# A mixer tile's gate products on VectorE: moved from ahead of the softmax maxima to behind them

## The chip, the cores and the metric

The kernel runs on one core of a Trainium2 chip. The metric is the device time of one execution in microseconds (us); it was measured in three runs, and one more execution was recorded by the hardware profiler. Engines are named as the profile names them: PE (TensorE's matmuls), PEld (its weight loads), DVE (VectorE), ACT (ScalarE), POOL (GpSimd), SP (SyncE, which issues most DMAs).

## What is computed

One decoder layer over 1024 tokens of width 1024, in f32. A first sub-layer mixes tokens: one input projection feeds (A) sliding-window attention of 8 query heads over 2 key heads (window 128, learned sinks) and (B) gated linear attention with 4 heads of 64 by 128. Their outputs are concatenated, projected and added to the input. A second sub-layer is a mixture of 32 experts, 4 for each token. Both are wrapped in norms and in shifts, scales and gates that come from a conditioning vector. The part that the change touches, cut from the reference:

```
s = jnp.where(valid, einsum(q, k) * scale, -inf)          # (A), a block of 128 tokens
m = jnp.maximum(jnp.max(s, -1), sink)
p = jnp.exp(s - m);  p = p / (sum(p) + jnp.exp(sink - m));  o = p @ v
...
b = jnp.cumsum(g, axis=2)                                  # (B), chunks of 64 tokens
A = einsum(q * jnp.exp(b - b_mid), k * jnp.exp(b_mid - b)) # masked to causal
o = A @ v + (q * jnp.exp(b)) @ states
kv = einsum(k * jnp.exp(b_last - b), v)                    # what a chunk adds to the state
```

## The kernel before

The program has three stretches: the projections of all tokens into the layouts that the mixer wants; a loop over eight tiles of 128 tokens that does both attentions (lines 682 to 719, about 164 to 392 us of the profiled span); and then the output projection, the router and the experts. Weights and activations of the big products are kept as a high and a low f16 half, so that one product is three matmuls (lines 149 to 151). Only the loop is touched.

A tile of the loop is written in this order. `gla_gates(t)` (line 534) makes the log gates (matmul L537, ACT L539 to L541, DVE L542), sums them within the chunks (matmul L546, ACT L552), takes differences on DVE (L553, L554) and exponentials on ACT (L555 to L558), and then, as its last part, multiplies the exponentials into the tile's queries and keys on DVE: ten instructions at L560 (a copy of the chunks' last decays), L563 (twice), L567 (four times), L570 (twice) and L573. They are called the products below. `project(t)` (line 509) makes the tile's linear-attention values and output gates: 96 matmuls into two PSUM buffers `pb`; the second goes through ACT L526, DVE L527, ACT L528 and L529, DVE L530. `ada_half(t)` (line 634) is POOL's work on the conditioning weights (L643 to L650), fed by DMAs that SP issues. `attention(t)` (line 456) has the scores in two rounds of four heads (matmuls L469 and L470), each round in two PSUM buffers `pss`; DVE adds the mask and takes the row maximum, head by head (L474); three short DVE instructions make the negative maximum and the sink's exponent (`nm` at L478 and L479, `es` at L481); ACT takes eight exponentials (L486). Then four rounds of transposes on PE (L495), copies out of PSUM by DVE (L501) or ACT (L499), products with the values (L504), and the division (L506). `gla(t)` (line 576) starts with the matmuls of the products with each other (L584, L585), masked copies on DVE (L588, L590), the matmuls L593 and L596, then the update of the state (L601 to L610) and the norm (L615 to L618).

Who sets the order: the source is traced, and the framework's scheduler then lays out one fixed queue for each engine, with the order of the source as priority and its own estimate of durations to decide what is ready. On the chip every queue runs in that order, and an instruction that has to wait holds up all behind it. The pool `psS` has two buffers `pss`, handed out in the order of the source: two for the gates of a tile, two and two for the rounds of scores, two for L584 and L585, one for the state's update. `tc.issue_after(ins)` adds to every instruction traced inside the block that is on the engine of `ins` an edge that puts it behind `ins` in that engine's queue.

Of the kernel before, what the change touches and what calls it, by code (L numbers as in the profile page):

```python
# [49 lines left out]
def layer_kernel(  # L50
# [4 lines left out]
    nc = tc.nc  # L55
# [118 lines left out]
    with tc.tile_pool(name="p1", bufs=1) as p1, tc.tile_pool(name="stage", bufs=4) as stage, \  # L174
# [211 lines left out]
        for t in range(NT):  # L386
            ps = psB.tile([128, 512], F32, name="pb")
            tk = slice(t * 128, (t + 1) * 128)
# [31 lines left out]
    with tc.tile_pool(name="p2", bufs=1) as p2, tc.tile_pool(name="wk", bufs=2) as wk, \  # L420
# [9 lines left out]
        sinkb = snk.rearrange("p i g -> p (i g)")  # L430
# [22 lines left out]
            for j in range(T, T + DUMP, 128):  # L453
                nc.sync.dma_start(yacc[j:j + 128, i * 512:(i + 1) * 512], am[0].rearrange("p a n -> p (a n)"))

        def attention(t, ao):
            w = 256 if t else 128
            k0 = (t - 1) * 128 if t else 0
            mx = wk.tile([128, 8], F32, name="mx")
            sms = []  # L460
            for i2 in range(2):
                sm = wk.tile([128, 4, 256], F32, name="sm")
                sms.append(sm)
                pss = [psS.tile([128, 2, 256], F32, name="pss") for _ in range(2)]
                for a in range(2):
                    for g in range(2):
                        i = 2 * i2 + a
                        tq, tk = slice(t * 128, (t + 1) * 128), slice(k0, k0 + w)
                        nc.tensor.matmul(pss[g][:, a, :w], qq[:, g, i, tq], kk[:, g, tk], start=True, stop=False)  # L469
                        nc.tensor.matmul(pss[g][:, a, :w], qq[:, g, i, tq], kl[:, g, tk], start=False, stop=True)  # L470
                for g in range(2):
                    for a in range(2):
                        h = 2 * (2 * i2 + a) + g
                        nc.vector.tensor_tensor_reduce(  # L474
                            sm[:, 2 * a + g, :w], pss[g][:, a, :w], amask[:, 256 - w:], op0=OP.add, op1=OP.max,
                            scale=1.0, scalar=-3e38, accum_out=mx[:, h:h + 1])
            nm = wk.tile([128, 8], F32, name="nm")
            nc.vector.scalar_tensor_tensor(nm, mx, SQK, sinkb, op0=OP.mult, op1=OP.max)  # L478
            nc.vector.tensor_scalar(nm, nm, -1.0, None, op0=OP.mult)  # L479
            es = wk.tile([128, 8], F32, name="es")  # L480
            nc.vector.tensor_add(es, sinkb, nm)  # L481
            nc.scalar.activation(es, es, AF.Exp)
            den = wk.tile([128, 8], F32, name="den")
            for h in range(8):
                sm = sms[h // 4][:, h % 4, :w]
                nc.scalar.activation(sm, sm, AF.Exp, scale=SQK, bias=nm[:, h:h + 1], accum_out=den[:, h:h + 1])  # L486
            nc.vector.tensor_add(den, den, es)
            rec = nc.vector.reciprocal(den, den)
            nk = w // 128
            po = psO.tile([128, 8, 64], F32, name="po")  # L490
            for i in range(4):
                pt = psT.tile([128, 4, 128], F32, name="pt")
                for g in range(2):
                    for b in range(nk):
                        nc.tensor.transpose(pt[:, g * nk + b, :],  # L495
                                            sms[i // 2][:, 2 * (i % 2) + g, b * 128:(b + 1) * 128], identf)
                pT = wk.tile([128, 4, 128], F32, name="pT")
                if i % 2:
                    nc.scalar.activation(pT[:, :2 * nk, :], pt[:, :2 * nk, :], AF.Copy)  # L499
                else:  # L500
                    nc.vector.tensor_copy(pT[:, :2 * nk, :], pt[:, :2 * nk, :])  # L501
                for g in range(2):
                    for b in range(nk):
                        nc.tensor.matmul(po[:, 2 * i + g, :], pT[:, g * nk + b, :],  # L504
                                         vv[:, t - nk + 1 + b, g * 64:(g + 1) * 64], start=b == 0, stop=b == nk - 1)
            nc.vector.tensor_tensor(ao, po, den[:, :, None].to_broadcast([128, 8, 64]), op=OP.mult)  # L506
            return rec

        def project(t, row):

# [23 lines left out]
        def gla_gates(t):  # L534
# [21 lines left out]
            nc.scalar.activation(ee[:, 0, :], ee[:, 0, :], AF.Exp)  # L556
            nc.scalar.activation(ee[:, 4, :], ee[:, 4, :], AF.Exp)
            nc.scalar.activation(bf, bf, AF.Exp)  # L558
            e3 = wk.tile([128, 2, 2], F32, name="e3")
            nc.vector.tensor_copy(e3.rearrange("p a c -> p (a c)"), ev[:, 2, :, 63])  # L560
            qk = ee.rearrange("p e (a n) -> p e a n", a=2)
# [9 lines left out]
                                        e3[:, :, 1 - c:2 - c].to_broadcast([128, 2, 64]), op=OP.mult)  # L571
            e4 = wk.tile([128, 2], F32, name="e4")
            nc.vector.tensor_tensor(e4, e3[:, :, 0], e3[:, :, 1], op=OP.mult)  # L573
            return ee, e4

        def gla(t, ee, e4, gv, sgg, go):
            A = am[t % 2]
# [104 lines left out]
        for t in range(NT):  # L682
            tk = slice(t * 128, (t + 1) * 128)
            row = ada_row(t // 2 - 1) if t and t % 2 == 0 else []

            wo = []
            for pc in range(t * 2, t * 2 + 2):
                cs = slice(pc % 8 * 128, (pc % 8 + 1) * 128)
                st = wos.tile([128, 4, 128], F32, name="wo", bufs=2)
                if pc >= 8:  # L690
                    wod = nc.sync.dma_start(st, w_out[512:1024, cs].rearrange("(i p) f -> p i f", p=128))
                else:
                    for g in range(2):
                        wod = nc.sync.dma_start(st[g * 64:(g + 1) * 64],
                                          w_out[g * 256:(g + 1) * 256, cs].rearrange("(i p) f -> p i f", p=64))
                ks = slice(pc // 8 * 4, pc // 8 * 4 + 4)
                wo.append((woh[:, ks, cs], wol[:, ks, cs], st))
            ao = wk.tile([128, 8, 64], F32, name="ao", bufs=1)
            gates = gla_gates(t)
            gv, sgg = project(t, row)  # L700
            with tc.issue_after(wod.ins):
                ada_half(t)
            rec = attention(t, ao)
            with tc.issue_after(rec.ins):
                for w in wo:
                    split(*w)
            aof = ao.rearrange("p h d -> p (h d)")
            pt = psT.tile([128, 4, 128], F32, name="pt")
            for i in range(4):
                nc.tensor.transpose(pt[:, i, :], aof[:, i * 128:(i + 1) * 128], identf)  # L710
            nc.scalar.activation(hTh[:, 0:4, tk], pt, AF.Copy, scale=SX)
            nc.vector.scalar_tensor_tensor(hTl[:, 0:4, tk], pt, SX, hTh[:, 0:4, tk], op0=OP.mult, op1=OP.subtract)
            go = wk.tile([128, 4, 128], F32, name="go", bufs=1)
            gla(t, *gates, gv, sgg, go)
            pt = psT.tile([128, 4, 128], F32, name="pt")
            for i in range(4):
                nc.tensor.transpose(pt[:, i, :], go[:, i, :], identf)
            nc.scalar.activation(hTh[:, 4:8, tk], pt, AF.Copy, scale=ggc)
            nc.vector.scalar_tensor_tensor(hTl[:, 4:8, tk], pt, ggc, hTh[:, 4:8, tk], op0=OP.mult, op1=OP.subtract)
# [764 lines left out]
```

## Time and profile before

| | us |
|---|---|
| three runs, median (lowest to highest) | 1987.58 (1984.33 to 1992.88) |
| the profiled execution, own time | 1980.73 |
| its span in the profile | 1978.6 |
| PE busy in the span | 1813.5 |
| DVE busy in the span | 1558.1 |

The span is the part that the profiler's records cover; 2.1 us of the profiled execution lie around it. All times inside the trace are from the span's start. A busy share says little of the whole here, since the stretches have different limits; what the change is worth has to be read from the loop.

### The profile page before, as it was taken

What the parts mean: (1) busy time and instruction counts of PE and PEld (TensorE: products, weight loads), DVE (VectorE), ACT (ScalarE), POOL (GpSimd) and SP (SyncE); (2) the same over time, 40 slices, a digit from 0 to 9 for tenths busy, and PEclk for the clock granted to TensorE, in tenths of its full rate; (3) what the DMA queues carried; (4) which work ended last, traced back from release to release, by engine and by line L of the source; (5) the groups of instructions that cost most, each with busy time, mean ns of one, the idle gap of its engine ahead of it and who ended that gap; (6) DMA issues with size and microseconds to landing.
All of it is one profiled execution on the core that took longest, in us unless ns stands there. A gap on an engine that the chain in (4) does not pass through costs nothing. (4 is left out here: it accounts for less than half of the span.)

```text
span 1978.6 us, 55425 instructions
## 1 busy us (share of the span) xinstructions
PE 1813.5 (92%) x22803; PEld 1587.7 (80%) x22803; DVE 1558.1 (79%) x2568; ACT 1305.4 (66%) x2247; POOL 1007.2 (51%) x989
## 2 busy tenths in 40 slices
PE   6999999989598999999999999999999999999980
PEld 3456887755398999999999997779889998999880
DVE  6824667666689989998998995779697978989873
ACT  5624555434376978878788785668577768868760
POOL 2204777646545656456565574436344535754441
PEclk9999999999699999999999999999999999999985
DMA  9412333333499999999999997689888989999983
GB/s 298 151 44 75 97 87 102 112 136 128 168 366 330 353 350 304 370 354 317 349 356 365 361 347 251 225 306 348 284 315 289 372 266 347 359 307 348 313 276 107
DMA packets 296630, 525.79 MB, mean 266 GB/s; under 512 B 19056, under 2 KB 79611, under 8 KB 296340
## 3 DMA queue, kind: packets, MB, share of 16 engines
q1 hardware_dynamic: 277682, 476.27, 69.1%
q0 software_dynamic: 17392, 41.72, 8.9%
q8 instruction: 180, 2.95, 0.6%
q10 hardware_dynamic: 1298, 4.21, 0.5%
q14 instruction: 78, 0.64, 0.1%
HBM read 482.37 MB, written 39.76 MB: 264 GB/s over the span
## 5 line engine op out<-in xcount | busy, mean ns | idle before, releaser
L171 DVE SCALAR_TENSOR_TENSOR el<-st,eh 128x1024 f16<-128x1024 f32 x768 | 934.7, 1240 | 91.2 <-ACT eh L170 89.2
L170 ACT ACTIVATE eh<-st 128x1024 f16<-128x1024 f32 x768 | 794.2, 1055 | 238.0 <-PE pu L150 133.6
L149 PE MATMUL pu<-xTh,eh 128*128 128x232 f16 (+31 forms) x4096 | 778.8, 231 | 7.6 <-DVE lin L1129 5.2
L150 PE MATMUL pu<-xTl,eh 128*128 128x232 f16 (+31 forms) x4096 | 777.8, 230 | 5.1 <-issue 4.9
L151 PE MATMUL pu<-xTh,el 128*128 128x232 f16 (+31 forms) x4096 | 777.9, 230 | 4.2 <-issue 4.2
L150 PEld LDWEIGHTS <-eh 128*128 128x128 f16 x6080 | 595.1, 99 | 42.0 <-issue 20.2
L149 PEld LDWEIGHTS <-eh 128*128 128x128 f16 x6080 | 592.8, 98 | 28.5 <-issue 6.6
L151 PEld LDWEIGHTS <-el 128*128 128x128 f16 x6080 | 592.5, 98 | 28.7 <-issue 6.8
L1132 POOL CAST aTh<-lin 128x232 f16<-128x232 f32 (+31 forms) x256 | 295.0, 1153 | 476.0 <-DVE lin L1131 411.0
L149 PE MATMUL pyv<-aTh,eh 128*128 128x232 f16 (+30 forms) x1984 | 375.4, 231 | 10.7 <-ACT yT L1159 6.7
L151 PE MATMUL pyv<-aTh,el 128*128 128x232 f16 (+30 forms) x1984 | 374.9, 231 | 1.5 <-issue 1.5
L150 PE MATMUL pyv<-aTl,eh 128*128 128x232 f16 (+30 forms) x1984 | 374.8, 230 | 0.8 <-issue 0.8
L1133 POOL TENSOR_TENSOR aTl<-lin,aTh 128x232 f16<-128x232 f32 (+31 forms) x256 | 271.2, 1060 | 20.6
L1129 DVE TENSOR_SCALAR lin<-pu,bt 128x232 f32<-128x232 f32 (+31 forms) x256 | 109.9, 429 | 71.8 <-PE pu L151 58.7
L1174 POOL DMA_INDIRECT yacc<-yo,tokI x52 | 94.4, 1815 | 114.7 <-ACT yo L1171 108.2
L1125 ACT ACTIVATE gl<-pu,bt 128x232 f32<-128x232 f32 (+31 forms) x256 | 98.1, 383 | 65.8 <-PE pu L151 35.1
L1130 DVE SCALAR_TENSOR_TENSOR lin<-lin,bt,sg 128x232 f32<-128x232 f32 (+31 forms) x256 | 105.2, 411 | 18.6 <-ACT sg L1127 4.6
L643 POOL TENSOR_TENSOR st<-st,sil 128x512 f32<-128x512 f32 x64 | 69.1, 1080 | 94.1 <-DMA st<-in_w_ada_dram 92.6
L1127 ACT ACTIVATE sg<-gl,c 128x232 f32<-128x232 f32 (+31 forms) x256 | 108.0, 422 | 1.0
L1087 POOL DMA_INDIRECT xg<-h2d,gatI x50 | 71.4, 1428 | 43.8 <-DVE gcol L1250 20.8
L1131 DVE SCALAR_TENSOR_TENSOR lin<-gl,lin 128x232 f32<-128x232 f32 (+31 forms) x256 | 83.6, 327 | 4.3
L1171 ACT ACTIVATE yo<-pxy,gcol 128x512 f32<-128x512 f32 (+26 forms) x104 | 70.3, 678 | 5.8 <-DMA yacc<-yo,tokI 5.8
(411 smaller groups left out, 2488.7 us busy)
## 6 DMA issues: line engine op xcount, KB each, us to landing
st<-in_w_mlp_dram SPq DMA_DIRECT2D x384, 1024.0 KB, 11.3
st<-in_w_ada_dram SPq DMA_DIRECT2D x64, 256.0 KB, 3.0
xt<-in_x_dram SPq DMA_DIRECT2D x16, 512.0 KB, 4.3
st<-in_w_ada_dram SPq DMA_DIRECT2D x16, 512.0 KB, 9.1
st<-in_w_in_dram SPq DMA_DIRECT2D x7, 1024.0 KB, 5.0
x1d<-xt SPq DMA_DIRECT2D x8, 512.0 KB, 2.6
h2d<-h2s SPq DMA_DIRECT2D x8, 512.0 KB
yacc<-yi ACTq DMA_DIRECT2D x8, 512.0 KB, 2.9
```

The source lines that it names most:

```text
L149: nc.tensor.matmul(ps, sh, mh, start=first, stop=False)
L150: nc.tensor.matmul(ps, sh, ml, start=False, stop=False)
L151: return nc.tensor.matmul(ps, sl, mh, start=False, stop=last)
L170: return (nc.scalar.activation(dh, src, AF.Copy, scale=SW), nc.vector.scalar_tensor_tensor(dl, src, SW, dh, op0=OP.mult, op1=OP.subtract))
L171: nc.vector.scalar_tensor_tensor(dl, src, SW, dh, op0=OP.mult, op1=OP.subtract))
L1125: nc.scalar.activation(gl, pu[0], AF.Relu, scale=-SG, bias=bc(0, j))
L1127: sgs.append(nc.scalar.activation(sg, gl, AF.Sigmoid, scale=-1.702 * INV / SG, bias=c7))
L1129: nc.vector.tensor_scalar(lin, pu[1], bc(1, j), bc(2, j), op0=OP.max, op1=OP.min)
L1130: nc.vector.scalar_tensor_tensor(lin, lin, bc(3, j), sg, op0=OP.add, op1=OP.mult)
L1132: nc.gpsimd.tensor_copy(aTh[:, j, :], lin)
L1133: lows.append(nc.gpsimd.tensor_tensor(aTl[:, j, :], lin, aTh[:, j, :], op=OP.subtract))
L1174: end["dma"] = nc.gpsimd.indirect_dma_start(out=yacc, out_offset=bass.IndirectOffsetOnAxis(ap=si(b)[:m, :], axis=0), in_=yo[:m, :], in_off ...
```

## The change

The ten products leave `gla_gates` and become a function of their own, `gla_products`, which `attention` calls behind `es`. They are thereby behind the tile's maxima in the source, so in priority, and `issue_after` puts them behind the `es` instruction of L481 in DVE's queue. No instruction is added or removed, no tile's size or number of buffers changes, no other engine's instruction is moved in the source.

```diff
-        def attention(t, ao):
+        def attention(t, ao, ee):
...
-            nc.vector.tensor_add(es, sinkb, nm)
+            top = nc.vector.tensor_add(es, sinkb, nm)
             nc.scalar.activation(es, es, AF.Exp)
+
+            with tc.issue_after(top.ins):
+                e4 = gla_products(t, ee)
             den = wk.tile([128, 8], F32, name="den")
...
-            return rec
+            return rec, e4
...
             nc.scalar.activation(bf, bf, AF.Exp)
+            return ee
+
+        def gla_products(t, ee):
+            tk = slice(t * 128, (t + 1) * 128)
+            ev = ee.rearrange("p e (a n) -> p e a n", a=4)
             e3 = wk.tile([128, 2, 2], F32, name="e3")
             nc.vector.tensor_copy(e3.rearrange("p a c -> p (a c)"), ev[:, 2, :, 63])
             qk = ee.rearrange("p e (a n) -> p e a n", a=2)
...
             nc.vector.tensor_tensor(e4, e3[:, :, 0], e3[:, :, 1], op=OP.mult)
-            return ee, e4
+            return e4
...
-            gates = gla_gates(t)
+            ee = gla_gates(t)
             gv, sgg = project(t, row)
             with tc.issue_after(wod.ins):
                 ada_half(t)
-            rec = attention(t, ao)
+            rec, e4 = attention(t, ao, ee)
...
-            gla(t, *gates, gv, sgg, go)
+            gla(t, ee, e4, gv, sgg, go)
```

## Rows read from the trace of the kernel before

**Rows 1.** The page's head: the span of the profiled execution.

```profile
span 1978.6 us, 55425 instructions
```

**Rows 2.** Windows: the eight tiles of the loop summed; the experts' stretch.

```profile
core 0: us, PE busy (x) PEld busy (x) DVE busy (x) ACT busy (x) POOL busy (x), PEclk, DMA share, GB/s
...
sum 227.60, PE 211.97 PEld 179.26 DVE 157.79 ACT 117.23 POOL 164.42; mean PE 26.50 PEld 22.41 DVE 19.72 ACT 14.65 POOL 20.55
...
545.00:1960.00 1415.00, 1337.40 (x19615) 1260.54 (x19613) 1213.44 (x1662) 1058.31 (x1604) 736.13 (x630) 0.98 0.95 322
```

**Rows 3.** Timeline of SP's queue: the first loads of expert weights.

```profile
527.50 3.54 SPq L1057 DMA_DIRECT2D st<-in_w_mlp_dram  x2
```

**Rows 4.** PE's waits in the loop, 164 to 392 us: total, times, longest.

```profile
PE pss L469 <- DVE mx L474: 8.4, 7, 2.5
PE pss L546 <- DVE az L542: 3.7, 3, 2.9
PE pt L495 <- ACT sm L486: 0.8, 3, 0.3
PE pt L677 <- DVE mx L675: 0.8, 1, 0.8
```

**Rows 5.** The first of these waits in tiles 3, 4, 5 and 7.

```profile
PE pss L469 <- DVE mx L474: 1.8, 1, 1.8
...
PE pss L469 <- DVE mx L474: 0.5, 1, 0.5
...
PE pss L469 <- DVE mx L474: 2.1, 1, 2.1
...
PE pss L469 <- DVE mx L474: 2.5, 1, 2.5
```

**Rows 6.** DVE timeline, tile 5: start, duration, line, operands, count, idle before.

```profile
309.61 0.67 DVE L563 TENSOR_TENSOR ee<-gkT,ee 128x256 f32<-128x256 f32 x1
...
311.22 1.12 DVE L570 TENSOR_TENSOR ee<-ee,e 128x128 f32<-128x128 f32 x1
...
314.16 0.41 DVE L527 TENSOR_SCALAR vg<-vg 128x512 f32<-128x512 f32 x1
```

**Rows 7.** PE timeline, tile 5: the second round of scores.

```profile
315.31 0.27 PE L469 MATMUL pss<-kk,qq 128*128 128x256 f16 x1 [2.09 <-DVE mx L474]
```

**Rows 8.** ACT timeline, tile 5: the activation ahead of L527.

```profile
311.51 0.60 ACT L526 ACTIVATE vg<-pb 128x512 f32<-128x512 f32 x1 [0.76 <-PE pb L151]
```

**Rows 9.** DVE timeline, tile 4, from the first product to the second copy.

```profile
281.78 0.60 DVE L563 TENSOR_TENSOR ee<-gkT,ee 128x256 f32<-128x256 f32 x1
...
284.06 0.28 DVE L570 TENSOR_TENSOR ee<-ee,e 128x128 f32<-128x128 f32 x1
284.26 0.15 DVE L573 TENSOR_TENSOR e<-e 128x2 f32<-128x2 f32 x1
...
285.84 0.80 DVE L527 TENSOR_SCALAR vg<-vg 128x512 f32<-128x512 f32 x1 [1.24 <-ACT vg L526]
...
290.68 0.44 DVE L588 COPY_PREDICATED am<-triu,pss 128x256 f32<-128x256 uint32 x1 [0.27 <-PE pss L585]
...
291.37 0.15 DVE L481 TENSOR_TENSOR es<-snk,nm 128x8 f32<-128x8 f32 x1
...
293.23 0.69 DVE L501 COPY pT<-pt 128x512 f32<-128x512 f32 x1 [0.55 <-PE pt L495]
295.68 0.69 DVE L501 COPY pT<-pt 128x512 f32<-128x512 f32 x1 [1.75 <-PE pt L495]
```

**Rows 10.** ACT timeline, tile 4: the first exponential.

```profile
291.22 0.51 ACT L486 ACTIVATE sm<-sm,nm 128x256 f32<-128x256 f32 x1 [3.25 <-DVE nm L479]
```

**Rows 11.** PE timeline, tile 4: the first reader of products, and a later one.

```profile
289.54 0.48 PE L584 MATMUL pss<-ee 64*128 64x128 f32 x2
...
295.91 0.61 PE L596 MATMUL po<-vg,am 128*128 128x128 f32 x4
```

**Rows 12.** POOL timeline, beside the slow L570 of tile 5.

```profile
311.11 1.08 POOL L643 TENSOR_TENSOR st<-st,sil 128x512 f32<-128x512 f32 x1 [1.11 <-DMA st<-in_w_ada_dram]
```

## The prediction

> **What bounds the kernel now.** I read the profile from the whole to the place. The span is 1978.6 us [rows 1], and the executed time of that execution 1980.73, so 2.1 us lie around it. The windows by stretch come next: in the eight tiles of the loop PE is busy 211.97 of 227.60 us, DVE only 157.79, ACT 117.23, POOL 164.42 [rows 2]. So the loop is bound by PE, which leaves 227.60 - 211.97 = 15.6 us idle, and nothing that is done to DVE can bring more than that there, unless PE's own work changed, which it does not. The experts' stretch is bound by PE too (1337.40 of 1415.00 us, [rows 2]); its first weights are issued at 527.50 [rows 3], 135 us behind the loop, behind routing that needs the loop's result. What the loop gains or loses therefore passes on to the end one for one.
>
> Then the view of PE's waits, cut to the loop, says what the idle time is [rows 4]: 8.4 us before L469, the second round of scores, which needs a `pss` buffer that the maxima of the first round still read; 3.7 us before L546, for the gates of the next tile; 0.8 and 0.8 us elsewhere. Together 13.7 us. The reader should see that the largest one is a wait for DVE, and that it is uneven: 1.8, 2.1 and 2.5 us in tiles 3, 5 and 7, but 0.5 us in tile 4 [rows 5].
>
> Why it is uneven stands in the timelines. In tile 5 DVE goes through the ten products from 309.61 to the start of L527 at 314.16, 4.55 us without a gap [rows 6]; the activation that L527 needs ended at 311.51 + 0.60 = 312.11 [rows 8], so L527 and the maxima behind it were 2.05 us late because of the products, and PE stood 2.09 us at L469 [rows 7]. In tile 4 the products took from 281.78 to 284.26 + 0.15 = 284.41, 2.63 us, and DVE then sat idle 1.24 us, waiting for ACT, ahead of L527 [rows 9]: there they were in nobody's way.
>
> **The change part by part.** *What is taken away from ahead of the maxima.* With the products gone, L527 of tile 5 starts at 312.11 and the maxima some 2.05 us earlier; L469, which started at 315.31 [rows 7], could start at 313.26, and PE had been idle since 315.31 - 2.09 = 313.22. The wait goes almost wholly. I take tiles 3 and 7 for the same pattern, since their waits are of the same size, and leave each tile the 0.5 us that tile 4 has with products that hindered nobody. Saved: 1.8 + 2.1 + 2.5 - 3 x 0.5 = 4.9 us. Bounds: nothing, if another thing is late next (it would be L526 itself, which waits for PE), and 8.4 us.
>
> *What is put behind `es`.* Ten DVE instructions in each of eight tiles, no DMA among them, and no other queue, SP's and POOL's included, has an instruction moved in the source. The cover is the time in which ACT takes eight exponentials: in tile 4 they begin at 291.22 [rows 10], `es` ends at 291.37 + 0.15 = 291.52, and DVE's copies for the transposes start at 293.23 and 295.68, with idle time before them [rows 9]. The masked copies L588 and L590, now partly between the maxima and `es`, must come behind the products, which brings `es` and the exponentials forward by about 0.6 us (0.44 us of L588 and 0.27 us of idle before it, [rows 9], less overlap). The ten then run from about 290.9 to 293.5 in tile 4's duration. The copy at 293.23 starts 0.3 us later; the products with the values behind it on PE wait as long, but PE has other work there. In tile 5's duration, 4.55 us, they end at 295.4, and the copy is 2.2 us late. DVE is not the bound, so its work as such costs nothing; if that cover is gone, it costs what PE waits.
>
> *The new wait.* L584 is the first reader of the products. It starts at 289.54 in tile 4 [rows 11], that is before `es`; now it can't start before about 293.5, 4 us later. Queued behind it on PE are the next tile's projection, the transposes and L596. The scheduler knows the dependency and fills PE with the 48 projection matmuls of the next tile that it now puts between, and L596 comes only at 295.91 [rows 11], so the 4 us are room that exists. What it does not know is how late DVE really is. Lower bound 0. Upper bound: the queue is laid out for durations like tile 4's, 2.63 us, and every tile takes tile 5's 4.55 us; then PE waits 4.55 - 2.63 = 1.9 us in each, 8 x 1.9 = 15.4 us. The nearest row is the wait for a result that comes out of the same place today, L495 for the exponentials: 0.8 us over the whole loop [rows 4]. I take 1 us.
>
> *What makes the products slow, and whether the new place cures it.* L570 of tile 5 started at 311.22, took 1.12 us [rows 6] and so ended at 312.34; POOL's L643 ran from 311.11 to 312.19 [rows 12]. The same line took 0.28 us in tile 4 [rows 9]: it was held until POOL was through, and then ran its usual length nearly. POOL is busy 164.42 of 227.60 us, 72% of the loop [rows 2], so a chain of ten meets it in the one place as in the other, and I count no change of its own from this. The Trainium skill, SBUF — State Buffer, section "SBUF: two separate sides", states the rule behind it: DVE with two inputs in SBUF and GpSimd share a pair of ports as an exclusive lock, and whoever comes second is blocked for the whole instruction. By that rule the ten are slow wherever POOL is at work, the late end of tile 5 would be the usual one, and the sum would be that of the second rival below; the rows show such holds in tile 5 and not in tile 4.
>
> *The sum.* -4.9 + 1.0 = -3.9 us. Against the profiled execution that is 1980.73 - 3.9 = 1976.8 us; this execution lies 6.9 us below the median of the runs shown, 1987.58, and the forecast is made against the median: 1987.58 - 3.9 = **1983.7 us**, 0.2% less.
>
> **The rivals.** A measurement of this kernel can tell about 0.5% from no change, 9.9 us.
>
> *All of PE's waits close.* With the maxima early, the whole tile moves forward, `az` (the 3.7 us) too, and PE runs without a named wait: -13.7 us, 1973.9. For it: DVE has 70 us free in the loop. Against it: the wait before L546 comes from work of the tile's end, which the change does not hurry, and tile 4 keeps 0.5 us with no product in the way.
>
> *The new wait takes the place of the old one, slower.* The place is L584 on PE, held by products that POOL holds up; PE's queue is in order, and tile 5 shows that it does not forgive 2 us of late DVE work [rows 6, 7]. The price is 15.4 us by the upper bound above, and the net -4.9 + 15.4 = +10.5: 1998.1 us. It turns from gain to loss where the wait is over 4.9 / 8 = 0.6 us in each tile, and it can be told from no change only where it is over (9.9 + 4.9) / 8 = 1.85 us. Against it: the scheduler may lay L584 out later than it must, and 4 us of projection stand ready.
>
> *The maxima do not come earlier.* The scheduler lays out PE's queue anew; it sees DVE free earlier, puts the second round of scores earlier too, and the wait stays as it is, for L527 and its ACT input: 0 us, 1987.6, or 1988.6 with the 1 us of the new wait. Tile 4 speaks for it, tiles 3, 5 and 7 against it.
>
> **How the numbers follow.** The forecast, a gain of some 1 to 8 us, gets 0.56; all waits closed 0.14; the slower one 0.15; no effect 0.15. Faster by over 0.5% is nearly all of the second case (0.13) and an upper end of the first (0.04): 0.17. Slower by over 0.5% is most of the slower case (0.12), and 0.02 for a layout that turns out worse in other ways: 0.14. The rest, 0.69, is within 0.5%. The range takes in the end of the closed waits (1973.9) and that of the slower rival (1998.1): 1973 to 1999; the likeliest case's own is 1979 to 1988.
>
> **What would show it.** In the profile of the changed kernel, PE's wait L469 <- L474 should fall from 8.4 to about 3.5 us, most in tiles 3, 5 and 7; the products should stand between L481 and the first L501 of each tile; the exponentials should start some 0.6 us sooner behind the maxima; a wait L584 <- product should be new and small, and L527 should follow L554 with only a wait for ACT between. I would be wrong if L584's wait were over 5 us in all, if PE's busy time in the loop changed, if the wait at L469 stayed, or if the time moved behind the loop, where I count nothing.

## The result, and the profile after

The median of the changed kernel is 2016.01 us (1994.87 to 2031.11, 13 runs), that of the kernel before, on the same chip, 1988.97 us (1977.60 to 1999.14, 13 runs): a ratio of 1.0113, interval 1.0089 to 1.0136. The ratio leaves out the three longest runs of the changed kernel (2025.13 to 2031.11 us), which lie over 1.5% above its fastest; the medians, with all runs, differ by 27.0 us. It is slower by more than the 0.5% that a measurement can tell, and outside the range given. The profiled execution took 2010.1 us, 29.4 more than that of before; the two lines of the page's head that matter are the span and the granted clock in 40 slices:

```profile
span 2008.3 us, 55412 instructions
...
PEclk9998888899869999999999999999999999999985
```

The loop has the whole of it. The timeline of SP's queue has the first load of expert weights at 559.25 instead of 527.50 us [rows 3], 31.8 later:

```profile
559.25 0.43 SPq L1065 DMA_DIRECT2D st<-in_w_mlp_dram  x1
```

Cut from the first difference of a tile's gates to the last writing of a mixer's result, the loop takes 258.9 us; cut in the same way it takes 227.4 us in the kernel before:

```profile
164.40:391.80 227.40, 211.76 (x1695) 179.18 (x1693) 157.59 (x459) 117.23 (x365) 164.42 (x261) 0.99 0.33 96
```

The windows of the kernel after, the loop first, then 14 us each from three of the falls described below, and 14 us of tile 3, where none came:

```profile
core 0: us, PE busy (x) PEld busy (x) DVE busy (x) ACT busy (x) POOL busy (x), PEclk, DMA share, GB/s
165.90:424.80 258.90, 241.76 (x1703) 203.32 (x1702) 156.71 (x459) 113.68 (x365) 163.54 (x261) 0.87 0.31 87
212.00:226.00 14.00, 13.48 (x60) 11.92 (x60) 5.61 (x14) 2.16 (x6) 6.61 (x10) 0.51 0.38 111
250.00:264.00 14.00, 13.84 (x62) 12.72 (x63) 5.12 (x11) 0.60 (x1) 8.47 (x11) 0.52 0.38 108
376.00:390.00 14.00, 14.00 (x63) 12.07 (x63) 5.77 (x17) 2.78 (x9) 6.27 (x11) 0.51 0.40 114
...
280.00:294.00 14.00, 12.37 (x97) 10.51 (x96) 8.72 (x21) 6.27 (x23) 5.66 (x8) 1.00 0.33 96
```

The reader should see two things. PE's busy time in the loop, 211.97 us in [rows 2], is now 241.76, with the same 22803 matmuls in the program: each takes longer. And the column PEclk says why. In the stretches from 212, 250 and 376 us it stands at 0.51 or 0.52, so nearly all of each ran at half clock (1.2 instead of 2.4 GHz), though PE is shown busy for 13.48 to 14.00 of 14 us; in the last row, of tile 3, PE is busy only 12.37 us and the clock is full. The clock record of the trace has five such stretches in the loop, called falls here: from 181.5 us for 10.2, and from 212.2, 249.8, 314.6 and 376.1 us for 13.7 each, 64.8 us in all. The kernel before had one of 3.4 us. If one half of the time at half clock is lost, that makes (64.8 - 3.4) / 2 = 30.7 us, against 258.9 - 227.4 = 31.5 measured. Reckoned at full clock, the two loops are about equally long: 258.9 - 32.4 = 226.5 and 227.4 - 1.7 = 225.7.

This holds beyond the one execution that was profiled, since every run has its span and its mean granted clock on record. Their product is the length that the span would have had at full clock throughout: its median is 1917.5 us in the 13 runs of the changed kernel (1909.4 to 1921.4) and 1914.6 to 1915.7 in the 74 runs of the kernel before that stood beside the experiments, on four chips. The spans themselves have medians of 2014.2 us against 1984.8 to 1988.8.

PE's waits in the loop, total, times and longest:

```profile
PE pss L593 <- DVE ee L575: 5.2, 5, 1.7
PE pt L498 <- ACT sm L489: 3.2, 6, 0.9
PE pss L469 <- DVE mx L474: 3.0, 5, 0.9
PE po L507 <- DVE pT L504: 2.3, 4, 1.1
PE pss L592 <- DVE ee L571: 1.9, 3, 1.3
PE pt L725 <- DVE go L626: 0.4, 1, 0.4
PE pss L549 <- DVE az L545: 0.2, 1, 0.2
```

The aimed-at wait went from 8.4 [rows 4] to 3.0 us, and that for `az` (now L549) from 3.7 to 0.2. But the first readers of the products (L592 and L593, before L584 and L585) wait 7.1 us, the products with the values 2.3, and the transposes (L498) 3.2 instead of 0.8. The sum is 16.2 against 13.7: even at full clock nothing was won.

Where a fall begins is seen in tile 2. DVE's timeline: start, duration, line, operands, count:

```profile
244.30 0.17 DVE L481 TENSOR_TENSOR es<-snk,nm 128x8 f32<-128x8 f32 x1
244.39 0.16 DVE L568 COPY e<-ee 128x4 f32<-128x4 f32 x1
...
245.13 1.33 DVE L575 TENSOR_TENSOR ee<-gkT,ee 128x128 f32<-128x128 f32 x2
246.38 0.81 DVE L578 TENSOR_TENSOR ee<-ee,e 128x128 f32<-128x128 f32 x1
247.11 1.59 DVE L575 TENSOR_TENSOR ee<-gqT,ee 128x128 f32<-128x128 f32 x2
...
249.43 0.68 DVE L504 COPY pT<-pt 128x512 f32<-128x512 f32 x1
```

POOL's timeline beside it:

```profile
244.94 1.17 POOL L651 TENSOR_TENSOR st<-st,sil 128x512 f32<-128x512 f32 x1 [1.43 <-DMA st<-in_w_ada_dram]
246.19 0.85 POOL L653 TENSOR_TENSOR st<-st 128x256 f32<-128x256 f32 x1
247.01 1.08 POOL L651 TENSOR_TENSOR st<-st,sil 128x512 f32<-128x512 f32 x1
```

PE's timeline, with the idle time before an instruction and its releaser in brackets:

```profile
246.25 0.38 PE L498 MATMUL pt<-identf,sm 128*128 128x128 f32 x2
248.29 0.44 PE L593 MATMUL pss<-ee 64*128 64x64 f32 x4 [1.67 <-DVE ee L575]
...
250.16 1.97 PE L507 MATMUL po<-vv,pT 128*128 128x64 f32 x8 [0.48 <-DVE pT L504]
...
255.40 3.52 PE L507 MATMUL po<-vv,pT 128*128 128x64 f32 x16
...
259.56 0.42 PE L151 MATMUL pb<-wvh,hTl 128*128 128x256 f16 x1
```

The two pairs of L575 took 1.33 and 1.59 us, where such a pair takes 0.48 to 0.53 with POOL cut (a_pool below). The first pair ended at 246.46, 0.35 us behind POOL's L651 (246.11), L578 at 247.19, 0.15 behind L653 (247.04), and the second pair at 248.70, 0.61 behind the next L651 (248.09): each got through only when POOL was done. So the products ran to 249.4 and longer; in the time that tile 4 had taken before, 2.63 us [rows 9], they would have ended at 247.0. PE stood 1.67 us before L593 and 0.48 before L507, and from 249.8 us the clock was at half: the eight L507 take 1.97 us and the f16 matmul 0.42, where the same took 1.10 and 0.27 at full clock. Six f16 matmuls came from 259.56, and at 263.4 the clock was back.

What PE did around these waits had changed as well. The scheduler's PE queue for one middle tile, one character for each matmul (`.` f16 projection, `s` attention scores, `G` L584 and L585 or their like, `t` transposes, `v` products with the values, `f` other f32 matmuls):

```
before: ssssssss........ssss...ssss........GGGG.GGGG....tt...tt..tt...tvvvvtttttffffvvvvvvvvttttff..vvvv........
after:  ssssssss........ssss...ssss......................tt.GGtt.ttGGttGGvvvvttttGGffvvvvvvvvtttt......vvvvfff
```

With the products late, the scheduler put 22 f16 matmuls in a row ahead of the transposes and had only two left for the passage behind them. From the first transposes to the next six f16 matmuls PE has, but for these two, only f32 matmuls in small tiles. This passage is called **the f32 run** below. A long row of them is not new: 32 stand there without any f16 matmul between them, and 28 did before. What is new is that the transposes and the products' readers ahead of that row have hardly any f16 matmul among them, where there had been a dozen, and that PE waits there.

### The profile page after: what moved, and what is told of

Its sections match the earlier page's. It is cut to its first block, busy times and chain, and to the rows that moved or that the text cites. A ratio compares the mean times of both kernels' runs of the same rounds, so it can differ in the third digit from the quotient of the medians.

```text
span 2008.3 us, 55412 instructions
## 1 busy us (share of the span) xinstructions
PE 1840.6 (92%) x22803; PEld 1608.8 (80%) x22803; DVE 1558.4 (78%) x2568; ACT 1301.9 (65%) x2247; POOL 996.0 (50%) x989
## 3 DMA queue, kind: packets, MB, share of 16 engines
q1 hardware_dynamic: 277682, 476.27, 68.3%
## 5 line engine op out<-in xcount | busy, mean ns | idle before, releaser
L1141 POOL TENSOR_TENSOR aTl<-lin,aTh 128x232 f16<-128x232 f32 (+31 forms) x256 | 257.8, 1007 | 20.6
L651 POOL TENSOR_TENSOR st<-st,sil 128x512 f32<-128x512 f32 x64 | 67.8, 1060 | 113.9 <-DMA st<-in_w_ada_dram 66.7
```

Source lines behind the costliest of these rows:

```text
L1141: lows.append(nc.gpsimd.tensor_tensor(aTl[:, j, :], lin, aTh[:, j, :], op=OP.subtract))
```

## The experiments

**Theory 1:** a fall needs both, the f32 run and a wait in it, and the waits come from products that POOL holds up. **The rivals:** the new order of PE's queue is enough by itself, or the waits are enough wherever they fall. The expectations have a third theory too, that the clock is a bystander and the chain of a tile has become longer. The loop is compared cut as above; *low* is its time at half clock by the clock record, and *at full* is its length less half of that.

| kernel | loop us | low us | at full | ratio to before (interval) |
|---|---|---|---|---|
| before | 227.4 | 3.4 | 225.7 | |
| after | 258.9 | 64.8 | 226.5 | 1.0113 (1.0089 to 1.0136) |
| a_pool | 214.7 | 0 | 214.7 | loop only |
| b_pool | 211.9 | 0 | 211.9 | loop only |
| b_late | 236.3 | 17.1 | 227.8 | 1.0014 (0.9985 to 1.0043) |
| a_split | 226.9 | 3.4 | 225.2 | 1.0007 (0.9983 to 1.0031) |
| a_dummy | 289.6 | 68.3 | 255.5 | 1.0161 (1.0111 to 1.0210) |
| a_reorder | 273.4 | 95.6 | 225.6 | 1.0108 (1.0054 to 1.0163) |
| a_weave | 236.8 | 23.9 | 224.9 | 1.0008 (0.9978 to 1.0039) |
| b_weave | 256.6 | 47.8 | 232.7 | 1.0142 (1.0088 to 1.0195) |
| b_half | 225.4 | 10.2 | 220.3 | 0.9979 (0.9949 to 1.0008) |
| b_dve | 232.7 | 17.1 | 224.2 | 1.0031 (1.0006 to 1.0056) |
| a_dve | 232.8 | 13.7 | 226.0 | 1.0069 (1.0038 to 1.0100) |
| a_weave_half | 230.0 | 13.7 | 223.2 | 1.0013 (0.9989 to 1.0037) |

The column *at full*, with the product of span and clock above, is the main evidence that the clock carries the difference, and it speaks against the third theory: where the conditioning is computed in full, it lies between 220.3 and 227.8 us in ten of twelve kernels, while the loop itself goes from 225.4 to 273.4. The two others (a_dummy, b_weave) have work or waits of their own. Each kernel was profiled once, so the loop of a single execution stands beside a ratio of several; where the two differ in size (a_reorder), the falls of other executions need not be those of the one profiled.

### a_pool: the changed kernel, POOL hardly there

POOL's conditioning products are cut to 8 of every 128 columns; the other columns are left out, so the router sends the tokens elsewhere and the stretches behind the loop are not compared.

```diff
+                    st = st[:, :, 0:8]
+                    acc = adac[:, pc * 128:pc * 128 + 8]
-                    nc.gpsimd.tensor_tensor(st, st, sil[...].to_broadcast([128, 4, 128]),
+                    nc.gpsimd.tensor_tensor(st, st, sil[...].to_broadcast([128, 4, 8]),
```

> The changed kernel with POOL's conditioning products cut to 8 of 128 columns (most of the conditioning is left out); the queues of PE and DVE keep the changed kernel's order. Theory 1 (waits): in the changed kernel PE waits 7 us in the loop for products that POOL holds up (L592, L593), inside a run of small f32 matmuls, and its clock falls to 1.2 GHz for some 13 us in five tiles; with POOL short the ten products take about 2.3 us, these waits fall under 2 us, the clock stays at 2.4 GHz in at least six of eight tiles, and the time is 1970 to 1988 us. Theory 2 (order): the clock falls because the f16 projection matmuls are used up ahead of a run of some 60 f32 matmuls, waits or not; it still falls in four or more tiles and the time stays 2003 to 2020 us. Theory 3 (chain): the clock is a bystander and the tile's chain is longer; the period of a tile stays above 30 us at full clock too.

The loop's window, with the columns of the windows above:

```profile
167.20:381.90 214.70, 212.28 (x1703) 177.95 (x1702) 129.06 (x460) 112.69 (x365) 57.11 (x261) 1.00 0.37 105
```

The clock is full throughout. PE's queue is in the same order as after the change, f32 run and all, but only one wait is left, 0.4 us at the tile's end. A group of products by line (count, busy time, mean ns) in the loop of the kernel after:

```profile
L578 DVE TENSOR_TENSOR ee<-ee,e 128x128 f32<-128x128 f32 x16 | 9.1, 566 | 0.0
```

and the same instructions here:

```profile
L579 DVE TENSOR_TENSOR ee<-ee,e 128x128 f32<-128x128 f32 x16 | 4.5, 280 | 0.0
```

The ten products of all tiles take 21.6 us, summed over their groups, instead of 36.5 (34.0 in the kernel before). So this order alone does not lower the clock, and the waits are gone with POOL's holds.

### b_late: the order without late products

The kernel before, with L584 and L585 put behind the last transpose of round 0 in PE's queue: nearly the order of after, an f32 run included, while the products are made early as before.

```diff
+                with tc.issue_after(turned[t].ins):
                     nc.tensor.matmul(pa[:, 0:128], qk[bs, 1, h // 2, :], ...)
```

> The kernel before, products in their old place, but the linear attention's score matmuls (L584, L585 of before) queued on PE behind the first transposes of the attention, so that PE's order is nearly the changed kernel's while the products are long done. Theory 1 (waits): PE has no wait for products, the clock stays at 2.4 GHz in at least six of eight tiles, time 1980 to 1995 us. Theory 2 (order): the clock falls in four or more tiles, time 2005 to 2025 us. Theory 3 (chain): the score matmuls come late here too, period above 30 us at full clock, 2000 to 2020 us.

PE's waits in the loop:

```profile
PE pss L471 <- DVE mx L476: 12.7, 7, 3.6
PE pt L722 <- DVE go L623: 3.1, 2, 2.7
```

The waits sum to as much as after the change (16.7 us), but only 0.9 us of them lie at the transposes: the large ones are at the second round of scores, among the f16 matmuls. The clock fell four times, for 3.4, 3.4, 6.8 and 3.4 us, each time within a wait of 2.7 to 3.6 us or close behind it, and never in the f32 run, which here has 35 f32 matmuls in a row. Waits twice as long as those in the run thus went with a quarter of the low time, and the total is not to be told from before. Theory 1 had expected at most two tiles with a fall; it got four short ones.

### a_split: the first readers' products early, the rest late

What L584 and L585 read (four products) is made in `gla_gates` again; the other six stay behind `es`.

```diff
+            for n, src in ((0, gqT), (1, gkT)):
+                nc.vector.tensor_tensor(qk[:, n], src[:, :, tk], qk[:, n], op=OP.mult)
+            for n, src, c in ((4, gkT, 0), (2, gqT, 1)):
...
+                nc.vector.tensor_tensor(qk[:, 3, :, cs], ...)
             return ee
...
-                for cch, to in ((c, 3), (1 - c, n)):
+                for cch, to in ((1 - c, n),):
```

> The changed kernel, but the four products that the linear attention's score matmuls read stay where they were before the change; the other six follow the sink's exponent. PE's queue is then the one of the kernel before. Theories 1 and 2 both expect no fall of the clock beyond the one of before; the wait of the second round of scores for the maxima falls from 8.4 to 4 to 6 us, since 1.6 of the 2.6 us of products in the way are gone; time 1978 to 1990 us. Theory 3 (chain): the copies for the transposes are still held up by six products, time 1990 to 2005 us.

PE's queue is that of before again, and so is the clock (3.4 us low). The waits add up to 12.0 us, 3.8 us at L507 among them, whose copies six products now hold up, as the third theory said; the longest is in tile 4:

```profile
300.13 1.10 PE L507 MATMUL po<-vv,pT 128*128 128x64 f32 x8 [1.95 <-DVE pT L504]
```

It stands at the head of a row of 28 f32 matmuls, behind the first of them, and the clock stayed full, as the 1.10 us show. So this wait ahead of a long row, with f16 matmuls right before it, brought no fall. The loop is 226.9 us, the ratio 1.0007; the median of 1992.65 us is a little above what theories 1 and 2 had expected, and the gain did not come. It is the four products that set the order of PE's queue, not the move as such.

### a_dummy: f16 matmuls added to the run

24 f16 matmuls of no use in each tile, six ahead of each group of L592 and L593, behind the first transposes.

```diff
+                with tc.issue_after(turned[t].ins):
+                    for k in range(6):
+                        nc.tensor.matmul(pa, identh, wvg[0][0][:, k, :], start=True, stop=True)
```

> The changed kernel with 24 f16 matmuls of 256 columns a tile added on PE inside the run of f32 matmuls; their results are overwritten and never read. They are 8 x 24 x 0.11 = 21 us of PE work at full clock. Theories 1 and 2: PE stays busy there, the clock falls in at most two tiles, and in spite of the added work the time is not above the changed kernel's: 1995 to 2012 us. Theory 3 (chain, the clock is a bystander): the added work comes on top, 2025 to 2045 us.

A miss: the clock was to stay up, and it was low for 68.3 us, three falls of 20.5 among them. Of PE's waits the longest was a new one, behind the added work:

```profile
PE po L511 <- DVE pT L508: 11.9, 6, 2.7
```

The median of 2025.88 us lies where the third theory had put it, but about 34 us of that, half of the 68.3, are the clock's and not the added work's. Adding f16 work is not a cure in itself. Nor is an unbroken row of f32 matmuls needed for a long fall: PE's timeline has no more than 14 of them in a row here. The three long falls came with waits like this one, at the first products with the values:

```profile
214.75 1.96 PE L511 MATMUL po<-vv,pT 128*128 128x64 f32 x8 [2.12 <-DVE pT L508]
```

Waits of 1.84 and 2.66 us at the same place went with falls of 3.4 us, and tile 3, without such a wait, had none.

### b_pool: the kernel before, POOL hardly there

The edit of a_pool on the kernel before, with the same columns left out.

> The kernel before with POOL's conditioning products cut to 8 of 128 columns (most of the conditioning is left out, so the routing and the time behind the loop are others; only the loop, from the first L553 to the last L719, is compared). The changed kernel with POOL cut took 214.7 us there, without a wait of PE and without a fall of the clock. Theory 1 (the cost of the change is POOL holding up the products): here the maxima no longer come late either, loop 216 to 224 us, so that with POOL out of the way the change is worth a gain of 1 to 9 us. Theory 2 (PE's new order is bad in itself): this loop is shorter than 214 us.

The window of its loop:

```profile
166.70:378.60 211.90, 208.85 (x1694) 178.80 (x1693) 129.63 (x459) 116.24 (x365) 56.06 (x261) 1.00 0.36 102
```

Without POOL's holds the products are in nobody's way even ahead of the maxima: the only named wait left is 0.8 us for `az`, and the loop is 2.8 us shorter than a_pool's 214.7. Theory 1 had expected 216 to 224 us here, and a gain by the change; the 211.9 is under the 214 that the rival had named. So the change gains nothing there either, and its order of PE's queue costs some 3 us by itself (PE is busy 208.85 us here and 212.28 in a_pool), without a fall of the clock and with one execution of each. POOL's share of the loop is 227.4 - 211.9 = 15.5 us in the kernel before and 258.9 - 214.7 = 44.2 after.

### a_reorder: the products that are read first, first

The four products that L592 and L593 read stand ahead of the other four large ones.

```diff
+                    if to == 3:
+                        four = nc.vector.tensor_tensor(*ops, op=OP.mult)
+                    else:
+                        rest.append(ops)
...
+            with tc.issue_after(four.ins):
+                for ops in rest:
+                    nc.vector.tensor_tensor(*ops, op=OP.mult)
```

> The changed kernel with the ten products in another order: the four that L592 and L593 read come first, the rest behind them. PE's queue is the changed kernel's but for a few places. Theory 1 (waits): the wait of L593 loses the two or three products that stood in front (0.28 to 1.1 us each), L592 and L593 wait 1 to 4 us in all instead of 7.1, the clock falls in at most three tiles instead of five, time 1990 to 2008 us. Theory 2 (the run of f32 matmuls by itself): falls and time as in the changed kernel, 2008 to 2022 us.

A miss for theory 1 in the form in which it stood: the waits were to shrink and the clock to come back. PE's waits:

```profile
PE pss L598 <- DVE ee L571: 5.3, 7, 1.3
PE pt L498 <- ACT sm L489: 4.0, 7, 0.8
...
PE pss L599 <- DVE ee L578: 1.8, 4, 0.9
```

The scheduler, which reckons with the earlier end, put the readers earlier too, and they wait 7.1 us again, now seven times at the first of them, where it was three. The clock fell in all eight tiles, for 95.6 us, with a median of 2014.29 us in the range of the rival, that the order is enough. The edit changed the order as well: PE's timeline has only one f16 matmul behind the first transposes, where there were two, and 36 f32 matmuls in a row instead of 32. So the sum of the waits does not set the low time: in tiles 3, 5 and 7 no wait at the transposes or the readers was over 0.5 us, and the clock fell for 13.7 us in each. A few tenths of a us in such a run went with a fall here, and without any wait there was none (a_pool; a_dve below, with 36 in a row); whether the longer row or the spread of the waits made the difference, this run does not tell.

### a_weave and b_weave: the f32 run taken apart

24 of the next tile's 48 first projection matmuls, which PE has to do anyhow, are queued in sixes behind each round's transposes.

```diff
+                with tc.issue_after(tr.ins):
+                    for step in ahead[2 * i:2 * i + 2]:
+                        step()
```

The changed kernel with it:

> The changed kernel with 24 of the next tile's 48 first projection matmuls (f16) queued in sixes behind the transposes of each round of the attention, so that PE's run of some 60 f32 matmuls is broken up; no work is added. The score matmuls of the linear attention then come at its end, when the products are long done. Theory 1 (waits on products start the fall): none is left, no fall of more than 4 us, loop 216 to 232 us, time 1976 to 1996 us. Theory 2 (the unbroken run keeps the clock low): the same. If neither holds and the late score matmuls lengthen the tile's chain (theory 3), the period of a tile is over 30 us at full clock and the time 2000 us or more.

The queue of a middle tile becomes, in the signs used above,

```
ssssssss.......ssss...ssss.................ttGGtt......ttttvvvv......tttt..vvvv....tvvvvttt......vvvvGGGGGG
```

and PE's longest wait is larger than any after the change:

```profile
PE po L510 <- DVE pT L507: 10.8, 6, 2.9
```

In the timeline one of these waits, with PE's instructions on either side:

```profile
297.11 0.60 PE L498 MATMUL pt<-identf,sm 128*128 128x128 f32 x4
300.06 1.10 PE L510 MATMUL po<-vv,pT 128*128 128x64 f32 x8 [2.35 <-DVE pT L507]
301.00 0.27 PE L149 MATMUL pb<-wvh,hTh 128*128 128x256 f16 x1
```

PE stood 2.35 us, longer than the 1.67 us at which the clock fell in tile 2 of after, and the eight matmuls behind it take 1.10 us: full clock. The two longest of the six waits at L510, 2.92 and 2.88 us, went with falls of 6.8 and 3.4 us, the other four with none. The kernel is back at the time of before, though its loop is above the 216 to 232 us expected. Of the 23.9 us at low clock, 13.7 are one fall in the last tile, which has no next tile to weave in. So waits as long as those of after do not bring its long falls where f16 matmuls stand between the groups; this is the counterpart of a_pool.

The kernel before with the same weave:

> The kernel before with the same weaving of projection matmuls, products in their old place. It separates what the weaving does alone: theory 1 expects the waits of the maxima to stay (6 to 9 us in all) and the time to be within 8 us of before, 1982 to 1998 us; the difference to the woven changed kernel is then what the move of the products is worth without a fall of the clock, 4 to 8 us by the prediction's own sum.

PE's largest wait there is

```profile
PE pb L149 <- DVE vg L550: 17.6, 5, 4.3
```

since the woven matmuls need a `pb` buffer that DVE, busy with the products, frees late. So 1.0142, over the 1982 to 1998 us expected, is no price of the products' move. But these waits answer a rival: they stand among f16 matmuls, and the clock fell all the same.

```profile
272.26 0.37 PE L149 MATMUL pb<-wvh,hTh 128*128 128x256 f16 x1 [4.34 <-DVE vg L550]
```

From 271.07 us, within this wait, the clock was at half for 13.7 us, though f16 matmuls followed at once. The waits of 4.10 and 3.93 us went with 13.7 and 10.2 us, those of 3.2 to 3.6 us with 3.4 us each. Waits of 4.1 and 4.3 us were thus enough here without an f32 run.

### b_half: shorter holds

POOL's two large instructions (L643, L645) in halves, in the kernel before.

```diff
+                    for j in range(2):
+                        js = slice(2 * j, 2 * j + 2)
+                        nc.gpsimd.tensor_tensor(st[:, js, :], st[:, js, :], ...
```

> The kernel before with POOL's two longer instructions (L643 of 1.04 us, L645 of 0.72 us) each cut into two halves; nothing is left out and PE's queue is the same. If what POOL costs the loop is the length of a single hold, the holds on DVE are about 0.5 us instead of up to 1.1, PE's wait for the maxima falls from 8.4 to 4 to 6 us, and the time is 2 to 5 us shorter than before, 1983 to 1988 us. If it is POOL's total time, which the cut does not lower, nothing changes: within 2 us of before.

The wait at L469 fell from 8.4 to 5.9 us, and 10.2 us at low clock were there instead of 3.4; 0.9979 with an interval that holds 1. The wait came out as expected, the gain did not show; on the total it is inconclusive.

### b_dve and a_dve: POOL's products on DVE

The conditioning's products move to DVE as fused multiply-adds at the end of a tile, in the kernel before and in the changed one. DVE gets 32 to 36 us more to do in the loop, and POOL has 2.3 us left. For b_dve neither of the expected outcomes came: its loop is 232.7 us, with 11.7 us of waits.

```diff
-                    nc.gpsimd.tensor_tensor(st, st, sil[...].to_broadcast([128, 4, 128]), op=OP.mult)
...
+                    for k in range(4):
+                        s = sil[:, kh * 4 + k:kh * 4 + k + 1]
...
+                            nc.vector.scalar_tensor_tensor(acc, st[:, k, :], s, acc, op0=OP.mult, op1=OP.add)
```

> The kernel before with the conditioning products of the loop moved from POOL to DVE (32 fused instructions a tile of about 0.2 to 0.3 us, so 51 to 77 us more DVE work in the loop) and to the end of the tile in the source; POOL has no work in the loop, so nothing holds DVE. The loop of the kernel before with POOL cut took 211.9 us instead of 227.4. If the holds were the cost, the loop is 212 to 222 us and the time 1975 to 1987 us. If DVE's own queue then is what is late, PE waits for DVE more than 14 us in the loop and the time is 1990 us or more.

> The changed kernel with the same move of the conditioning products from POOL to DVE: no hold by POOL, all outputs computed. Theory 1 (the change's loss needs POOL's holds): PE waits under 3 us for products at the score matmuls and its clock falls in at most two tiles; the time is within 6 us of the kernel before with the same move. Theory 2 (the run of f32 matmuls alone): the clock falls in four or more tiles and the time is 15 us or more above it.

The medians are 1996.09 and 1997.57 us: with nothing to hold the products, the change costs 1.5 us instead of 27. PE's first waits in the loop of a_dve have no product among them:

```profile
PE pt L498 <- ACT sm L489: 5.0, 3, 3.5
PE pss L469 <- DVE mx L474: 2.9, 4, 1.4
```

Its one fall in the loop, 13.7 us from 376.3, begins within the longest of these, 3.5 us up to 378.57, at the transposes of tile 7: at the f32 run again, with another cause. In the other tiles PE's timeline has up to 44 f32 matmuls in a row, with no wait among them, at full clock. That POOL's holds make the loss is shown here with the whole computation left in place, as theory 1 had expected it; the two intervals overlap, so the 1.5 us are no measured difference.

### a_weave_half: weave and halves together

The changed kernel with both edits, to see whether something better than the kernel before comes out.

> The changed kernel with both mends together: 24 projection matmuls of the next tile woven into the run of f32 matmuls, and POOL's two longer instructions cut into halves; nothing is left out. The woven kernel alone had a loop of 236.8 us, of which 23.9 us at the lower clock, and PE waits of 10.8 us for the copies behind the products. If shorter holds bring these waits down, to 5 to 8 us, the loop is 222 to 232 us and the time 0.1 to 0.6% under before, 1975 to 1986 us; if POOL's total time decides, it stays where the woven kernel is, within 0.3% of before.

1993.02 us, 1.0013: as fast as before, not faster, so the gain that shorter holds were to bring did not come. No version was found that beats it.

## Why the prediction was wrong

**The product holds: right.** The prediction let POOL's overlap stand as a price that the products pay "in the one place as in the other". They do: 34.0 us for all of them before, 36.5 after, 21.6 with POOL cut. The Trainium skill, SBUF — State Buffer, section "SBUF: two separate sides", states an exclusive lock on a port pair that DVE and GpSimd share; 280 ns against 566 for the same instruction agrees. Two readings were loose, though neither enters the sum: behind POOL's end L570 of tile 5 ran 0.15 us more, about half of its usual 0.28, and the experts' stretch, read as bound by PE, has a DMA share of 0.95 in the same row.

**The saving at L469: right in place and size.** 8.4 fell to 3.0 us, 5.4 saved against 4.9 expected, nearly all of it in tiles 3, 5 and 7. That the loop passes on to the end one for one held too: 31.5 us in the loop, 29.7 at the end of the span. The 3.7 us for `az` went too, which only the first rival had.

**"The new wait", 1 us: wrong, the mis-sized term of the sum.** It measured 5.2 + 1.9 = 7.1 us at the first readers, and to that come 2.3 at L507 behind them and 3.2 - 0.8 = 2.4 at the transposes ahead of them, which wait for ACT's exponentials and come right behind the 22 f16 matmuls now. The step that failed took the scheduler's filling of PE as room ("fills PE with the 48 projection matmuls"). It is, as far as the scheduler knows durations; it lays the readers out for products that nobody holds, and moves them forward as soon as the products look earlier (a_reorder). The price from a quiet tile was no price for tiles in which POOL works: tile 2 took 5.0 us from L568 to the copy L504. By the waits alone, the sum would have been 16.2 - 13.7 = +2.5 us, no measurable change.

**"Unless PE's own work changed, which it does not": wrong, and this is the 30 us.** The number of matmuls didn't change, their order did, and with it the clock. All rivals priced waits as waits; the slower one had the right place (L584) and the right holder (POOL), but its 15.4 us upper bound counted idle time alone. The prediction itself named a change of PE's busy time as what would make it wrong, and had 0.02 for "a layout that turns out worse in other ways". The windows of the kernel before have the column that would have raised the question: PEclk was 0.99 over the loop with 13.7 us of waits in it, so that waits seemed harmless to the clock. They stood among f16 matmuls, and only the longest, 2.9 us at L546, was followed by a fall, of 3.4 us. It is just these matmuls that the change moves.

The Trainium skill, TensorE: Matmul & The Clock Gate, section "A second HAM failure mode: psum-queue depth-cycling", describes a kernel whose clock goes to and fro between its two levels since PE idles briefly between groups of matmuls. The trace of after agrees in kind, with 1.67 us of idling in tile 2. The runs add that the same or longer waits do less or nothing elsewhere (3.6 us in b_late, 2.35 in a_weave, 1.95 in a_split).

**What is shown, and what stays open.** Shown is that with holds gone (a_pool, a_dve), or with f16 matmuls that PE must do anyhow put between the groups (a_weave), or with the old order (a_split), the falls go or nearly go; and that the loop at full clock is about the same. So the loss of this change needs both the waits that POOL's holds make and the order that lost its f16 matmuls. As a rule for every fall, theory 1 does not hold: waits of 4.1 and 4.3 us among f16 matmuls went with long falls too (b_weave), and so did waits of 2.12 us where the f32 matmuls are broken up (a_dummy).

Not shown is how long a wait must be, nor what around it counts. Tiles 3, 5 and 7 of after kept the clock, with no wait over 1.09, 0.29 and 0.40 us in their runs, while 1.67 us went ahead of the fall in tile 2; but in a_reorder waits of 0.5 us and less were enough. Nor why the dummy matmuls of a_dummy did not help where the woven ones of a_weave did. A wait put into the run with POOL idle was not tried.

## What to carry to other kernels

Before moving producers in a program whose queues a scheduler lays out, look at what the scheduler will draw forward to fill the gap, and what is then missing where it was taken from: here f16 matmuls of the next tile's projection, among which PE had waited with hardly a loss of its clock. When PE's busy time rises with the same number of matmuls, read PEclk by stretch first, and compare loops as length less half of the time at low clock. A DVE chain that runs beside large POOL instructions is to be priced from tiles in which POOL is at work, not from the quiet ones.

## What was not expected of the hardware

PE was shown busy for 13.48 to 14.00 of 14 us while its granted clock was at 1.2 GHz: a full busy column is no sign of a full clock. A wait of 1.67 us in a passage of small f32 matmuls was followed by 13.7 us at half clock, a wait of 3.6 us among f16 matmuls by 6.8 (b_late), one of 4.34 us by 13.7 (b_weave), and a wait of 2.35 us close to f16 matmuls on either side by none (a_weave). The clock came back in tile 2 only 3.9 us behind the start of the next f16 matmuls, and 24 f16 matmuls added to each tile's run did not keep it up (three falls of 20.5 us).
